# Differential attention's v projection moved into the stretch where GQA attention is woven with MLA, and new costs in the scheduler that orders the program

## The chip, the cores and the metric

One NeuronCore of a Trainium2 chip runs the whole kernel. It has a matrix engine (TensorE, "PE" in the rows), a vector engine (VectorE, DVE), a scalar engine (ScalarE, ACT), GpSimd (POOL), and SyncE (SP), which here issues the DMA transfers. Each engine works through its own instructions in the order in which the program has them, and waits for another through semaphores. The metric is the device time of one execution in microseconds. Less is better.

## The reference

Two requests of 512 and 256 tokens go through the same two-layer encoder trunk, of width 1024, in fp32. Cut to what matters:

```
def layer(x, c, l, p, pos, row, col):
    shift, scale, gate = split(silu(c) @ ada_w[l] + ada_b[l], 3)
    h = rms_norm(x, norm_g[l]) * (1 + scale) + shift
    qa, kva, kra, ga, qb, kb, vb, gb, xc, gc, qd, kd, vd, gd = split(h @ w_in[l])
    oa = mla_branch(qa, kva, kra, ...)   # latents normed, then up-projected to q, k, v; softmax attention
    ob = diff_branch(qb, kb, vb, ...)    # per head o1 - lam * o2, two softmax attentions with one v; rms_norm
    oc = rglru_branch(xc, ...)           # conv, two gates, linear recurrence in both directions
    od = gqa_branch(qd, kd, vd, ...)     # qk-norm, rotary, softmax attention, 4 q heads on 2 kv heads
    o = concat([oa*silu(ga), ob*silu(gb), oc*silu(gc), od*silu(gd)])
    return x + gate * (o @ w_out[l])

def trunk(x, c, p):            # once for the 512 tokens, once for the 256
    for l in range(2): x = layer(x, c, l, p, ...)
    return rms_norm(x, final_norm)
```

In the changed part `vb` is the 256 columns of `h @ w_in` that are differential attention's v.

## The kernel before

**Tiles.** The 768 tokens are six tiles of 128: group 0 has tiles 0 to 3 and group 1 has tiles 4 and 5. The normed input `h` stays in SBUF for a whole layer, with features on partitions, as eight chunks of 128 features. fp32 precision comes out of faster fp32r matmuls: each operand is split into a high part and a low rest, and `mm3` (its matmuls stand under L285) forms each product by three matmuls. A weight that arrives by DMA is split on chip: ACT copies the high part (`wh`) and DVE or POOL subtracts it to get the low part (`wl`, L211).

**Projections.** `token_chunk(ci)` projects one block of `w_in` to a token-major result, one token tile after the other, with 24 matmuls (8 chunks times 3) for each tile and one `yield` after it. Block 2 is differential attention's v (256 columns), 3 its q, 4 its k, and 5 MLA's latents (320 columns). `feat_tile` does the same for feature-major results: the RG-LRU input and the gates. `v_evac` brings a finished v tile from PSUM to SBUF, by two high copies on ACT and two subtractions on DVE (L460) for each tile.

**The program of a layer.** Work is written as generators, and `take` and `weave` interleave them. `weave(jobs, fill, per, ...)` writes an attention's jobs (scores, softmax, transposed probabilities, product with v) and, between them, steps of the generator `fill`. A fixed number, `F_D` for the first weave with one value for each layer, says how many steps come per job. The order of a layer is:

1. GQA's projections, whole;
2. GQA attention, filled with `mla()`: six tiles of latents, then up-projections;
3. MLA attention, filled with gate projections and the adaptive-norm weights;
4. RG-LRU and differential attention's projections by turns: `take(lru, 2)`, `take(df, 6)` (v), `take(lru, 2)`, `take(df, 6)` (q), `take(lru)`, `take(df)` (k). RG-LRU works in two halves of 128 channels, `ct` 0 and 1;
5. differential attention, filled with gates and weights; then the output projection.

**The order that runs.** The written order is only the input of `arrange`, a list scheduler that runs when the program is built. It takes, over all engines, the ready instruction that can start first by its own clock (between equals, the one written first), with `_cost` for the durations and `REACH` for the latency between engines. An instruction that opens a tile must find a free buffer of its pool (`acc` 2, `s` 2, `tr` 3 and `pv` 1 in PSUM; `ws` 4, `wh` 6 and `wl` 6 for weights), and a pool hands its buffers out in written order. The result fixes every engine's order, so a wrong cost shows as an engine that waits in order for something that comes late.

**Where things stand.** L520 is the softmax's row maximum on DVE, L764 differential attention's score matmuls, L622 the transposes of its rotated q and k, L460 and L463 (DVE) the low parts of what is brought out of PSUM. `stacks` then sends those to their places by small DMAs (L750, L752). The RG-LRU's sums are L993 to L1009 (DVE).

Of the kernel before, what the change touches and what calls it, by code (L numbers as in the profile page):

```python
# [10 lines left out]
F32 = mybir.dt.float32  # L11
# [3 lines left out]
AF = mybir.ActivationFunctionType  # L15
# [58 lines left out]
def body(ctx, tc, I, O, dbg=None):  # L74
# [312 lines left out]
    for l in range(DEPTH):  # L387
# [330 lines left out]

        def diff():
            both, Vs = v_tiles(4)  # L720

            def evac_v(tt, acc):
                v_evac(both, tt, acc)
            yield from token_chunk(2, evac_v)
            qr = sb([P, NT, 256], tag="rot")
            kr = sb([P, NT, 256], tag="rot")
# [28 lines left out]
            def job(g, cp, half, j, o, dens, after):  # L755
                n = GRP[g][1]
                st = {}

                def soft():
                    st["P"] = []  # L760
                    for h2 in range(n // 256):

                        (p1, d1), (p2, d2) = [softmax(
                            lambda out, qt: nc.tensor.matmul(out, q[:96, qt * P:(qt + 1) * P], k[:96], start=True,  # L764
                                                             stop=True), g, h2, d) for (q, k), d in
                            zip(st["qk"], (dens[:, 2 * h2:2 * h2 + 2, 2 * half + j], None))]
                        V.reciprocal(d2, d2)
                        V.scalar_tensor_tensor(d2, d2, nlam, d1, op0=ALU.mult, op1=ALU.mult)
                        for i in range(2):
                            V.scalar_tensor_tensor(p1[:, i], p2[:, i], d2[:, i:i + 1], p1[:, i],  # L770
                                                   op0=ALU.mult, op1=ALU.add)
                        st["P"].append(p1)
                        yield

                def pv():
                    yield from transpose_pv(st["P"], g, Vs[2 * half + j], lambda pv: o_evac(o, j, pv, n))
# [59 lines left out]

        def mla(ahead):
            lat = [pair(g) + pair(g) + pair(g) for g in range(2)]
# [30 lines left out]
            for tt, _ in enumerate(token_chunk(5, evac, ahead)):  # L869
# [193 lines left out]

        lru, gq = rglru(), gqa()
# [154 lines left out]
def _cost(i):  # L1219
# [6 lines left out]
    if kind == "InstMatmult":  # L1226
        n, cols, f32 = size(i.ins[0]), size(i.ins[1]), i.ins[0].dtype == F32
        if not f32:
            return max(n * 0.45 + 4, 118), n / 2.4 + 172
        if cols <= 64 and n > 128:  # L1230
            return n / 1.2 + 30, n / 0.6 + 160
        if n == 128:
            return 110, 273
        return (215, 362) if n < 128 else (n / 0.6 + 8, n / 0.6 + 170)
# [3 lines left out]
    if eng == mybir.EngineType.Activation:  # L1238
        s = 0.84 * n + (50 if psum else 92)
        if i.func not in (AF.Copy, AF.Square):  # L1240
            s += 110
        if len(outs) > 1:
            s += 90
        return s, s + 100
    if eng == mybir.EngineType.Pool:
        return 2.3 * n + 90, 2.3 * n + 135
    if kind in ("InstTensorScalarPtr", "InstTensorCopy") and not psum and len([a for a in ins if size(a) == n]) == 1:
        s = 0.66 * n + 70
    else:
        s = 1.04 * n + 65  # L1250
    return s, s + 80


REACH = {"PE": 54.0, "Activation": 35.0, "DVE": 33.0, "Pool": 78.0, "SP": 27.0}


def arrange(tc):
# [4 lines left out]
    for k, i in enumerate(prog):  # L1262
# [12 lines left out]
        for name, acc in touched.items():  # L1275
# [5 lines left out]
            users.setdefault(name, []).append(k)  # L1281
        deps.append(d - {k})
    users = {t: u for t, u in users.items() if tiles[t]._space != bass.MemoryType.DRAM}
    free, queue, opens, left = {}, {}, {}, {}
# [7 lines left out]
    for t, u in users.items():  # L1292
        for k in u:
            closes.setdefault(k, []).append(t)
    cost = [_cost(i) for i in prog]
    n = len(prog)
    after = [[] for _ in range(n)]
# [8 lines left out]
    at, came, end, freed = dict.fromkeys(REACH, 0.0), [0.0] * n, [0.0] * n, {}  # L1306
    dma, column, order = 0.0, None, []

    def buffers(k):
# [9 lines left out]
    while len(order) < n:  # L1319
        best = None  # L1320
        for e, ks in ready.items():
            for k in ks:
# [15 lines left out]
        if e == "PE":  # L1338
# [144 lines left out]
```

## Time and profile before

| | |
|---|---|
| runs of the kernel before | 964.23 us median of 3 (960.71 to 964.87) |
| profiled execution | 965.95 us, span 964.1 us |
| mean granted TensorE clock | 0.974 |
| PE busy | 889.8 us, 92% of the span |
| DVE busy | 730.8 us, 76% |
| ACT busy | 560.5 us, 58% |
| POOL busy | 153.7 us, 16% |

The span runs from the first to the last instruction of the profiled execution. "Busy" is the sum over an engine's instructions without overlaps. A matmul's end is modelled, so a row's duration is longer than the distance to the next matmul where they follow closely: the starts tell more than the durations.

### The profile page before, as it was taken

What the parts mean: (1) busy time and instruction counts of PE and PEld (TensorE: products, weight loads), DVE (VectorE), ACT (ScalarE), POOL (GpSimd) and SP (SyncE); (2) the same over time, 40 slices, a digit from 0 to 9 for tenths busy, and PEclk for the clock granted to TensorE, in tenths of its full rate; (3) what the DMA queues carried; (4) which work ended last, traced back from release to release, by engine and by line L of the source; (5) the groups of instructions that cost most, each with busy time, mean ns of one, the idle gap of its engine ahead of it and who ended that gap; (6) DMA issues with size and microseconds to landing.
All of it is one profiled execution on the core that took longest, in us unless ns stands there. A gap on an engine that the chain in (4) does not pass through costs nothing.

```text
span 964.1 us, 15513 instructions
## 1 busy us (share of the span) xinstructions
PE 889.8 (92%) x5248; PEld 726.4 (75%) x5248; DVE 730.8 (76%) x1894; ACT 560.5 (58%) x1355; POOL 153.7 (16%) x168
## 2 busy tenths in 40 slices
PE   4799989999999898998999999999999999998996
PEld 1598767686899566776888977777688887786785
DVE  5688988766498476879557899998556876998746
ACT  5544888766446354657336368988437535687412
POOL 0221011003121010113201111000032212010610
PEclk9899999999999798999999999999999999998999
DMA  9721012222202654236610112020331214323502
GB/s 347 264 72 55 1 66 66 65 61 84 66 23 80 178 161 161 68 88 240 222 56 34 45 55 66 2 66 18 106 108 45 66 59 123 94 59 129 175 23 109
DMA packets 54351, 91.72 MB, mean 95 GB/s; under 512 B 9072, under 2 KB 13936, under 8 KB 54272
## 3 DMA queue, kind: packets, MB, share of 16 engines
q1 hardware_dynamic: 54272, 90.73, 30.0%
q8 instruction: 42, 0.69, 0.3%
q14 instruction: 37, 0.30, 0.1%
HBM read 73.38 MB, written 6.31 MB: 83 GB/s over the span
## 4 chain that ended last, share of the span: by engine, by line
PE 49%; DVE 25%; ACT 11%; DMA 7%; issue 6%; SPq 1%; POOL 1%; DVEq 0%; ACTq 0%; POOLq 0%
PE acc L285 22%; PE tr L285 9%; PE s L285 7%; ACT p L114 4%; DVE mx L520 3%; PE pv L539 3%; DVE pt L460 2%; DMA b<-ada 2%; ACT b L114 2%; PE tr L535 2%; DVE p L770 2%; DVE b L460 2%; PE s L764 1%; DMA p<-x 1%; ACT tmp L114 1%
## 5 line engine op out<-in xcount | busy, mean ns | idle before, releaser
L285 PE MATMUL acc<-b,wh 128*128 128x512 f32 (+1 forms) x576 | 159.5, 358 | 0.0
L285 PE MATMUL acc<-wh,b 128*128 128x256 f32 (+4 forms) x720 | 158.0, 308 | 0.2 <-DVE b L1020 0.2
L211 POOL TENSOR_TENSOR wl<-ws,wh 128x512 fp32r<-128x512 f32 (+3 forms) x56 | 78.7, 1408 | 416.6 <-ACT wh L114 372.3
L114 ACT ACTIVATE p<-s,mx 128x512 f32<-128x512 f32 (+1 forms) x192 | 117.9, 616 | 46.0 <-DVE mx L520 37.1
L285 PEld LDWEIGHTS acc<-wh,b 128*128 128x128 f32 (+1 forms) x720 | 118.3, 190 | 3.8 <-DVE b L1020 1.2
L285 PE MATMUL acc<-wl,b 128*128 128x256 f32 (+4 forms) x360 | 112.7, 315 | 4.6 <-DVE rs_y L164 1.7
L285 PEld LDWEIGHTS acc<-b,wh 128*128 128x128 f32 x576 | 102.8, 195 | 13.5
L285 PE MATMUL acc<-b,wl 128*128 128x512 f32 (+1 forms) x288 | 104.3, 362 | 0.0
L520 DVE TENSOR_REDUCE mx<-s 128x1 f32<-128x512 f32 x128 | 86.4, 682 | 21.1 <-PE s L764 19.8
L539 PE MATMUL pv<-pt,b 128*128 128x512 f32 (+1 forms) x288 | 88.2, 393 | 8.8 <-DVE pt L460 7.5
L460 DVE TENSOR_TENSOR pt<-tr,pt 128x512 fp32r<-128x512 f32 (+1 forms) x144 | 84.2, 593 | 9.2 <-ACT pt L114 8.6
L114 ACT ACTIVATE pt<-tr 128x512 fp32r<-128x512 f32 (+1 forms) x144 | 74.2, 524 | 21.9 <-PE tr L535 21.1
L535 PE MATMUL tr<-c,p 128*128 128x128 f32 x480 | 77.9, 281 | 5.3 <-DVE p L770 2.5
L114 ACT ACTIVATE wh<-ws 128x512 fp32r<-128x512 f32 (+3 forms) x100 | 62.9, 636 | 32.6 <-PE tr L285 15.9
L285 PE MATMUL tr<-wh,b 128*128 128x256 f32 (+2 forms) x432 | 81.3, 288 | 0.0
L535 PEld LDWEIGHTS tr<-c,p 128*128 128x128 f32 x480 | 58.5, 143 | 24.5 <-DVE p L770 4.7
L285 PEld LDWEIGHTS acc<-wl,b 128*128 128x128 f32 (+1 forms) x360 | 68.1, 190 | 8.5 <-ACT pt L114 3.0
L539 PEld LDWEIGHTS pv<-pt,b 128*128 128x128 f32 x288 | 47.0, 193 | 34.9 <-DVE pt L460 22.4
L285 PEld LDWEIGHTS tr<-wh,b 128*128 128x128 f32 x432 | 67.4, 189 | 0.7
L285 PEld LDWEIGHTS acc<-b,wl 128*128 128x128 f32 x288 | 56.2, 195 | 8.1 <-issue 1.7
L285 PE MATMUL tr<-wl,b 128*128 128x256 f32 (+2 forms) x216 | 62.3, 288 | 0.0
L114 ACT ACTIVATE b<-tr 128x128 fp32r<-128x128 f32 (+7 forms) x92 | 39.5, 447 | 34.6 <-PE tr L622 11.6
(254 smaller groups left out, 1879.9 us busy)
## 6 DMA issues: line engine op xcount, KB each, us to landing
ws<-wf SPq DMA_DIRECT2D x40, 256.0 KB, 3.0
b<-ada SPq DMA_DIRECT2D x32, 256.0 KB, 5.4
ws<-wt SPq DMA_DIRECT2D x32, 256.0 KB, 2.9
wh<-ada SPq DMA_DIRECT2D x32, 256.0 KB, 3.5
wl<-ada SPq DMA_DIRECT2D x32, 256.0 KB, 3.7
ws<-wo SPq DMA_DIRECT2D x32, 256.0 KB, 2.7
b<-b SPq DMA_DIRECT2D x112, 64.0 KB, 2.0
b<-b SPq DMA_DIRECT2D x112, 32.0 KB, 1.9
```

The lines of the kernel that those rows point to most:

```text
L114: return nc.scalar.activation(out, in_, f, **kw)
L211: engine(eng).tensor_tensor(lo, w, hi.bitcast(F32), op=ALU.subtract)
L285: nc.tensor.matmul(out, s, m, start=first and i == 0, stop=last and i == 2)
L460: V.tensor_tensor(lo, src, hi.bitcast(F32), op=ALU.subtract)
L520: V.tensor_reduce(mx[:, i:i + 1], views[i], axis=AX.X, op=ALU.min)
L535: nc.tensor.transpose(tr[:, qt * P:(qt + 1) * P], Ps[qt // 2][:, qt % 2, kt * P:(kt + 1) * P], ident)
L539: nc.tensor.matmul(pv[:, :n], vt(g, kt), p[:, :n], start=(kt == 0 and i == 0), stop=(kt == nk - 1 and i == 1))
L764: lambda out, qt: nc.tensor.matmul(out, q[:96, qt * P:(qt + 1) * P], k[:96], start=True, stop=True), g, h2, d) for (q, k), d in
L770: V.scalar_tensor_tensor(p1[:, i], p2[:, i], d2[:, i:i + 1], p1[:, i], op0=ALU.mult, op1=ALU.add)
```

## The change

**The move.** v's projection becomes a generator of its own, `diff_v`. `mla` gets it as `between` and runs it after the latents of all six tiles and before the up-projections, so that it is written into GQA attention. `F_D` rises, since the fill has six steps more. In stage 4 the turns are now lru 2, q, lru 2, k, lru's rest: k's projection is written ahead of RG-LRU's last part.

**The scheduler's costs.** Several durations are refitted. A PE instruction whose operand comes late gets a penalty (`LOAD`, by its form), a transpose that another form follows gets 82 ns back, matmuls take longer while the scheduler believes the clock to be halved, and two instructions of DVE and POOL that touch only SBUF block each other (`shared`, `port`). The lines of the clock's model are left out below.

No instruction is added or removed: both programs have 5086 instructions on PE, 1896 on DVE, 1104 on ACT, 173 on POOL and 536 on SP.

```diff
-F_D, F_A, F_B, F_C = ((0.897, 1.178), (0.494, 0.213), (1.2, 1.393), (1.833, 0.976))
+F_D, F_A, F_B, F_C = ((1.4, 1.6), (0.494, 0.213), (1.2, 1.393), (1.833, 0.976))
...
-        def diff():
-            both, Vs = v_tiles(4)
+        def diff_v():
+            both, dv["Vs"] = v_tiles(4)
 
             def evac_v(tt, acc):
                 v_evac(both, tt, acc)
             yield from token_chunk(2, evac_v)
+
+        def diff():
             qr = sb([P, NT, 256], tag="rot")
...
-        def mla(ahead):
+        def mla(ahead, between):
...
+            yield from between
             qr = [sb([P, NT, 192], tag="rot") for _ in range(2)]
...
-        fill = mla(token_load(5) if PRE_D[l] else None)
+        fill = mla(token_load(5) if PRE_D[l] else None, vg)
...
         take(lru, 2)
         take(df, 6)
         take(lru, 2)
-        take(df, 6)
+        take(df)
         take(lru)
-        take(df)
...
+LOAD = {"r": 100.0, "t": 55.0, "n": 30.0, "c": 0.0}
...
-                key = (max(at[e], s + REACH[e] if s else 0.0), k)
+                r = s + REACH[e] if s else 0.0
+                if e == "PE":
+                    a = at[e] - (82 if pform == "t" != form[k][0] else 0)
+                    key = (max(a, r + LOAD[form[k][0]] if r > pst + 30 else 0.0), k)
+                else:
+                    key = (max(at[e], r), k)
...
+        elif shared[k]:
+            other = port["Pool" if e == "DVE" else "DVE"]
+            for a, b in other[-6:]:
+                if a < s + 60 < b:
+                    slot, took = max(slot, b - 140 + slot - s), max(took, b - 140 + took - s)
+            port[e].append((s, s + took))
```

**What moves: PE, layer 0, from MLA's latents to its first up-projection.** In the rows of an order a tile's name has its number; `acc_1770` is the last tile of latents, `kvl` and `kvh` are up-projection weights, and L704/L705 are GQA's scores. Before, the up-projection (`acc_1894`) follows the latents at once:

```order
L285 MATMUL acc_1770<-wl_1237,b_535 128x320
L285 MATMUL acc_1770<-wh_1235,b_535 128x320 x2
L285 MATMUL acc_1770<-wl_1237,b_543 128x320
L285 MATMUL acc_1770<-wh_1235,b_543 128x320 x2
...
L704 MATMUL s_1875<-b_1164,b_1170 128x256
L705 MATMUL s_1875<-b_1164,b_1170 128x256
L285 MATMUL acc_1894<-kvl_1846,b_1210 128x256
L285 MATMUL acc_1894<-kvh_1844,b_1211 128x256
L285 MATMUL acc_1894<-kvh_1844,b_1210 128x256
```

In the changed kernel v's matmuls (`acc_2106`, weights of 256 columns) stand in between, one by one between GQA attention's transposes (L535) and its scores, and the first up-projection (`acc_2178`) comes among the last of them:

```order
L285 MATMUL acc_2106<-wl_1784,b_503 128x256
L535 MATMUL tr_2152<-c_83,p_2018 128x128
L285 MATMUL acc_2106<-wh_1782,b_503 128x256
L535 MATMUL tr_2152<-c_83,p_2018 128x128
L285 MATMUL acc_2106<-wh_1782,b_503 128x256
...
L704 MATMUL s_2210<-b_1178,b_1184 128x256
L285 MATMUL acc_2106<-wl_1790,b_519 128x256
L285 MATMUL acc_2178<-kvl_1727,b_1194 128x256
L285 MATMUL acc_2106<-wh_1788,b_519 128x256
L285 MATMUL acc_2178<-kvh_1725,b_1195 128x256
```

All of v's 144 matmuls of a layer (6 tiles of 24) have left the stretch after MLA attention. Over the whole program, 570 of 780 transposes were followed by another transpose; now 83 are.

**DVE, layer 0, where differential attention begins.** L460 and L463 split the first transposed q and k, which `stacks` sends on by DMA; L1006 to L1009 (L1009 to L1012 in the changed kernel's numbering) are the end of RG-LRU's second half, with the sums in `b_3796` and `b_4006`; L735 to L740 rotate k. Before, the splits came after k's rotations, and RG-LRU had been done long before:

```order
L1008 SCALAR_TENSOR_TENSOR p_3730<-p_3731,p_3730 128x512
L1008 SCALAR_TENSOR_TENSOR p_3764<-p_3765,p_3764 128x256
L1009 TENSOR_TENSOR b_3796<-b_3796,p_3730 128x512
L1009 TENSOR_TENSOR b_3428<-b_3428,p_3764 128x256
...
L737 TENSOR_TENSOR t_947_4012<-rot_3514,c_85 128x64
L740 TENSOR_TENSOR rot_3514<-t_946_4010,t_947_4012 128x8x8
L460 TENSOR_TENSOR b_4026<-tr_4020,b_4025 128x512
L463 SCALAR_TENSOR_TENSOR b_4035<-tr_4029,b_4034 128x512
...
L520 TENSOR_REDUCE mx_4141<-s_4142 128x1
```

In the changed kernel they stand behind the last sums of RG-LRU, and L463 behind the very last:

```order
L1009 TENSOR_TENSOR p_3974<-p_3974,p_3973 128x512
L1011 SCALAR_TENSOR_TENSOR p_3940<-p_3941,p_3940 128x512
L1010 SCALAR_TENSOR_TENSOR b_3640<-p_3975,p_3974 128x256
L1012 TENSOR_TENSOR b_4006<-b_4006,p_3940 128x512
L1011 SCALAR_TENSOR_TENSOR p_3974<-p_3975,p_3974 128x256
L460 TENSOR_TENSOR b_4026<-tr_4020,b_4025 128x512
L1012 TENSOR_TENSOR b_3640<-b_3640,p_3974 128x256
L463 SCALAR_TENSOR_TENSOR b_4035<-tr_4029,b_4034 128x512
...
L520 TENSOR_REDUCE mx_4141<-s_4142 128x1
```

On PE, the transposes for these splits follow the last matmul of RG-LRU's second half at once. From that matmul to the first scores stand, in layer 0, 14 matmuls of 512 columns, 24 of 256, 8 transposes, and 8 matmuls of the adaptive norm (L226); in layer 1, 35 of 512, 26 of 256 and 16 transposes. Before, the transposes came right behind the last matmul of k, and RG-LRU's last matmul stood among k's first tiles.

**DVE, at the start.** L319 and L320 make the normed input's high and low parts, L233 to L247 compute the adaptive norm's scale and shift, L406 to L419 prepare small tables of layer 0, and L211 are low parts of weights. Before:

```order
L320 TENSOR_TENSOR b_377<-tmp_374,b_376 128x512
...
L233 COPY tmp_411<-acc_402 128x512
L241 TENSOR_TENSOR adaB_93<-tr_413,c_81 128x8
L406 TENSOR_TENSOR lp_559<-pt_549 128x64
...
L419 TENSOR_SCALAR subS_567<-subS_567 128x256
L233 COPY tmp_428<-acc_419 128x512
...
L211 TENSOR_TENSOR wl_595<-ws_591,wh_593 128x512
L245 TENSOR_TENSOR adaA_92<-tr_430,c_81 128x8
L246 TENSOR_SCALAR adaA_92<-adaA_92 128x8
```

In the changed kernel the tables stand ahead of L233, and two more weight splits (`wl_827`, `wl_833`) ahead of the last scale (L245):

```order
L406 TENSOR_TENSOR lp_559<-pt_549 128x64
L408 TENSOR_REDUCE ls_561<-lp_559 128x2
L400 TENSOR_TENSOR pt_554<-rot_551,pt_549 128x4x64
...
L419 TENSOR_SCALAR subS_567<-subS_567 128x256
L211 TENSOR_TENSOR wl_589<-ws_585,wh_587 128x512
...
L233 COPY tmp_411<-acc_402 128x512
L241 TENSOR_TENSOR adaB_93<-tr_413,c_81 128x8
L233 COPY tmp_428<-acc_419 128x512
L211 TENSOR_TENSOR wl_827<-ws_823,wh_825 128x576
L211 TENSOR_TENSOR wl_833<-ws_829,wh_831 128x576
L245 TENSOR_TENSOR adaA_92<-tr_430,c_81 128x8
L246 TENSOR_SCALAR adaA_92<-adaA_92 128x8
```

## Rows read from the trace of the kernel before

**Rows 1.** The page's busy times: engine, us (share of the span), number of instructions.

```profile
PE 889.8 (92%) x5248; PEld 726.4 (75%) x5248; DVE 730.8 (76%) x1894; ACT 560.5 (58%) x1355; POOL 153.7 (16%) x168
```

**Rows 2.** Busy times by stretch: us; PE, PEld, DVE, ACT, POOL; PEclk, DMA, GB/s.

```profile
83.00:152.00 69.00, 62.34 (x371) 50.88 (x369) 63.91 (x222) 55.07 (x159) 8.54 (x15) 1.00 0.14 43
152.00:228.80 76.80, 74.31 (x422) 55.11 (x423) 58.61 (x135) 54.60 (x136) 8.08 (x17) 1.00 0.25 73
228.80:311.30 82.50, 79.44 (x591) 74.34 (x590) 61.22 (x119) 42.87 (x85) 18.08 (x16) 1.00 0.18 55
556.00:632.00 76.00, 69.71 (x412) 58.17 (x411) 70.49 (x249) 60.25 (x178) 10.42 (x22) 0.98 0.14 44
632.00:702.50 70.50, 68.13 (x381) 49.15 (x379) 53.01 (x111) 49.91 (x123) 6.26 (x11) 1.00 0.22 67
702.50:783.00 80.50, 78.28 (x583) 73.39 (x581) 60.27 (x110) 43.51 (x82) 19.23 (x17) 1.00 0.20 60
```

**Rows 3.** The chain that ended last, 236 to 260 us: start, us, what.

```profile
240.21 2.84 PE acc L285 x24
...
254.75 0.30 DVE b L460
```

**Rows 4.** PE's timeline, the last matmuls of RG-LRU's second half, layer 0.

```profile
295.78 0.62 PE L285 MATMUL tr<-b,pt 128*128 128x256 f32 x3
```

**Rows 5.** DVE's timeline, layer 0: RG-LRU's last sums, and the second split.

```profile
307.24 1.00 DVE L1009 TENSOR_TENSOR b<-b,p 128x512 f32<-128x512 f32 x2
...
313.46 0.68 DVE L463 SCALAR_TENSOR_TENSOR b<-tr,b 128x512 fp32r<-128x512 f32 x1
```

**Rows 6.** The page's DMA issues: count, KB each, us to landing.

```profile
b<-b SPq DMA_DIRECT2D x112, 64.0 KB, 2.0
```

**Rows 7.** PE's timeline, start of differential attention, layer 0: start, us, line, tiles, shapes.

```profile
311.39 1.04 PE L622 MATMUL tr<-c,rot 128*128 128x128 f32 x8
312.18 0.47 PE L285 MATMUL acc<-b,wl 128*128 128x512 f32 x1
312.49 0.62 PE L285 MATMUL acc<-b,wh 128*128 128x512 f32 x2
312.95 0.40 PE L285 MATMUL acc<-b,wl 128*128 128x512 f32 x1
...
324.41 1.19 PE L764 MATMUL s<-b,b 96*128 96x512 f32 x2 [3.60 <-DMA b<-b]
```

**Rows 8.** PE's timeline at the start: the adaptive norm's matmuls (L226) and last row sums.

```profile
29.53 2.26 PE L226 MATMUL acc<-b,c 128*32 128x512 f32 x16
...
39.49 1.57 PE L236 MATMUL tr<-c,tmp 128*128 128x2 f32 x8 [4.28 <-DVE tmp L233]
```

**Rows 9.** PE's timeline, start of differential attention, layer 1; in brackets idle time and releaser.

```profile
786.19 0.33 PE L622 MATMUL tr<-c,rot 128*128 128x128 f32 x1 [2.16 <-DVE rot L740]
```

**Rows 10.** Busy times by stretch, two stretches at half clock; columns as in rows 2.

```profile
323.10:340.10 17.00, 15.34 (x46) 9.08 (x47) 8.57 (x17) 5.34 (x14) 0.00 (x0) 0.50 0.62 191
...
787.00:791.00 4.00, 4.00 (x12) 3.10 (x12) 2.51 (x7) 1.44 (x2) 0.00 (x0) 0.57 0.48 161
```

**Rows 11.** PE's timeline, 47 us on: transposes (L312) between matmuls.

```profile
47.14 0.28 PE L285 MATMUL s<-wh,b 128*128 128x256 f32 x1
47.26 0.38 PE L312 MATMUL tr<-c,p 128*128 128x128 f32 x2
47.39 0.36 PE L285 MATMUL s<-wh,b 128*128 128x256 f32 x1
47.59 0.28 PE L285 MATMUL s<-wl,b 128*128 128x256 f32 x1
```

**Rows 12.** DVE's timeline, same start in layer 1: rotations during POOL's splits, and after.

```profile
784.58 1.30 DVE L737 TENSOR_TENSOR t<-rot,c 128x64 f32<-128x64 f32 x1
...
786.31 0.22 DVE L737 TENSOR_TENSOR t<-rot,c 128x64 f32<-128x64 f32 x1
```

**Rows 13.** POOL's timeline, same start in layer 1.

```profile
781.88 3.92 POOL L211 TENSOR_TENSOR wl<-ws,wh 128x512 fp32r<-128x512 f32 x3 [18.14 <-ACT wh L114]
```

More of the change, by code (lines that the diff above doesn't have):

```diff
@@ L775, in pv @@
                 def pv():
-                    yield from transpose_pv(st["P"], g, Vs[2 * half + j], lambda pv: o_evac(o, j, pv, n))
+                    yield from transpose_pv(st["P"], g, dv["Vs"][2 * half + j], lambda pv: o_evac(o, j, pv, n))
                     after()
@@ L1062, in weave @@
                     next(fill, None)
-        lru, gq = rglru(), gqa()
+        dv = {}
+        lru, gq, vg = rglru(), gqa(), diff_v()
         rot_acc[:] = ROT_A
@@ L1228, in _cost @@
         if not f32:
[L1229 removed]
+            return max(n * 0.443 + 4, 117), n / 2.4 + 172
         if cols <= 64 and n > 128:
[L1231 removed]
+            return n / 1.2 + (55 if cols == 64 else 8), n / 0.6 + 160
         if n == 128:
[L1233 removed]
+            return 109, 273
         return (215, 362) if n < 128 else (n / 0.6 + 8, n / 0.6 + 170)
@@ L1238, in _cost @@
     if eng == mybir.EngineType.Activation:
-        s = 0.84 * n + (50 if psum else 92)
-        if i.func not in (AF.Copy, AF.Square):
-            s += 110
+        s = 0.845 * n + (64 if psum else 98)
+        if i.func == AF.Identity or i.func in (AF.Exp, AF.Tanh) and not psum:
+            s += 185
+        elif i.func in (AF.Exp, AF.Tanh):
+            s += 89 if i.func == AF.Exp else 44
         if len(outs) > 1:
-            s += 90
+            s += 92
         return s, s + 100
     if eng == mybir.EngineType.Pool:
-        return 2.3 * n + 90, 2.3 * n + 135
-    if kind in ("InstTensorScalarPtr", "InstTensorCopy") and not psum and len([a for a in ins if size(a) == n]) == 1:
-        s = 0.66 * n + 70
+        return 2.38 * n + 80, 2.38 * n + 125
+    single = len([a for a in ins if size(a) == n]) == 1 and not psum
+    if kind == "InstTensorCopy" and single:
+        s = 0.545 * n + 68
+    elif kind == "InstTensorScalarPtr" and single:
+        s = 0.62 * n + 78
     else:
-        s = 1.04 * n + 65
+        s = 1.03 * n + 78
     return s, s + 80
 REACH = {"PE": 54.0, "Activation": 35.0, "DVE": 33.0, "Pool": 78.0, "SP": 27.0}
+LOAD = {"r": 100.0, "t": 55.0, "n": 30.0, "c": 0.0}
+WINDOW = 3413.0
 def arrange(tc):
@@ L1295, in arrange @@
     cost = [_cost(i) for i in prog]
+    form, shared = [None] * n_prog, [False] * n_prog
+    for k, i in enumerate(prog):
+        if eng[k] == "PE":
+            w, f32 = int(np.prod([c for _, c in i.ins[0].ap[1:]])), i.ins[0].dtype == F32
+            form[k] = "r" if not f32 else "t" if w == P else "n" if w < 32 else "c", w * (2 if f32 else 1) / 2.4
+        elif eng[k] in ("DVE", "Pool"):
+            shared[k] = not any(hasattr(a, "ap") and a.bass_ap.tensor._space == bass.MemoryType.PSUM
+                                for a in list(i.ins) + list(i.outs))
     n = len(prog)
@@ L1307, in arrange @@
     dma, column, order = 0.0, None, []
+    port = {"DVE": [], "Pool": []}
+    pst, pform, slow, busy, wend = -1e9, None, 2.0, 0.0, WINDOW
     def buffers(k):
@@ L1343, in arrange @@
                 s += 92
-            column = (pos, s + took - 10) if pos else None
+            fm, beats = form[k]
+            while s >= wend:
+                slow = (1.0 if busy >= 0.46 * WINDOW else 2.0) if slow == 1 else (1.0 if busy >= 0.81 * WINDOW else 2.0)
+                busy, wend = 0.0, wend + WINDOW
+            slot, took = slot + (slow - 1) * beats, took + (slow - 1) * beats
+            column = (pos, s + took - 10) if pos else None
+            pst, pform = s, fm
+            x = s
+            while s + slot > wend:
+                busy += wend - x
+                slow = (1.0 if busy >= 0.46 * WINDOW else 2.0) if slow == 1 else (1.0 if busy >= 0.81 * WINDOW else 2.0)
+                x, busy, wend = wend, 0.0, wend + WINDOW
+            busy += s + slot - x
+        elif shared[k]:
[4 more added lines that the diff above has]
+            port[e].append((s, s + took))
         if e == "SP":
```

1 line of the change is left out of this document (added).

## The prediction

> **What bounds the kernel now.** I read the page's busy times first, then busy times by stretch, then the chain that ended last, then PE's and DVE's timelines where a stretch begins. The page shows PE busy for 889.8 us [rows 1]; the profiled execution took 965.95 us. No other engine is near that, so PE's stream of matmuls and the places where it waits make the time. The stretches say where it waits [rows 2]. In layer 0, the one with GQA attention and MLA (83 to 228.8 us) leaves PE idle for 6.66 + 2.49 = 9.15 us; the one with RG-LRU's and differential attention's projections (228.8 to 311.3) for 3.06 us. In layer 1 the same stretches show 6.29 + 2.37 = 8.66 us and 2.22 us. The early part of the attention stretch, where the latents and up-projections hang on each other, is also DVE's fullest: 63.91 of 69 us, and 70.49 of 76 in layer 1. So the change takes work out of a nearly dense stretch and puts it into one with gaps. What it is worth depends on how much of it falls into these gaps, and on what the dense stretch was hiding.
>
> **v's matmuls leave the projections.** The chain passes through v's tiles whole, at 2.84 us for each 24 matmuls [rows 3]. Six tiles are 17.0 us in each layer, all on the path that sets the end: -34.0 us.
>
> **They arrive in GQA attention.** They need only `h` and weights, so they can stand in any gap where PE would wait for a softmax or a latent, and they put 144 matmuls between latents and up-projections, which wait for each other today. Their evacuation is 12 subtractions on DVE of 0.30 us [rows 3], 3.6 us beside 126 of it in 155 us, and is hidden. Two bounds. If every idle microsecond is filled, the stretch grows by 17.0 - 9.15 = 7.85 us in layer 0 and 8.34 in layer 1. If it only gets as dense as the projections are now, 79.44 of 82.5, or 96.3%, its 136.65 + 17 us of PE's work take 159.6 us, which is 13.8 more than now; in layer 1 (137.84 + 17 at 78.28 of 80.5, 97.2%) 12.7 more. PE's busy time counts modelled ends, so the second bound is too dark. I take 9.5 us each, nearer to the first, because the new matmuls depend on nothing that is late: +19.0, between 16.2 and 26.5. The move's net is -15.0, between -17.8 and -7.5.
>
> **The start of differential attention.** This is what the dense stretch was hiding. Before, RG-LRU's second half ended under k's projection: its last matmuls ended at 296.40 [rows 4], its last sums at 308.24 [rows 5], 11.8 us later, with PE busy throughout. Now k is projected first. The orders show the transposes of q and k right behind RG-LRU's last matmul, and on DVE both low-part splits behind its last sums. So the splits end 11.8 + 0.68 + 0.68 = 13.2 us after that matmul. The transfers that bring the split parts to their places follow. One takes 2.0 us from issue to landing [rows 6]; the order has two more at SP behind it before the scores' tiles are whole, and I add half as much again for these: 3.0 us, an estimate. The first scores can start 16.2 us after RG-LRU's last matmul. PE has this much to do until then: in layer 0, 14 x 0.23 + 24 x 0.118 + 8 x 0.10 us [rows 3, 7] is 6.9, and 8 matmuls of the adaptive norm cost between 0.14 (16 of them in 2.26 us, four at a time [rows 8]) and, alone among others, perhaps 0.5 each. That makes 8.0 to 10.9, and I take 9.5. PE waits 6.7 us, where it waited 3.60 [rows 7]: +3.1. In layer 1, 35 x 0.23 + 26 x 0.118 + 16 x 0.10 is 12.7 us, so it waits 3.5, where it waited 2.16 [rows 9]: +1.3. The half clock that follows such a wait is there already, 17.0 us at 0.50 in layer 0 and about 3.4 us at half in layer 1 [rows 10]; I add nothing for it. Below, the bound is no extra wait (0); above, the transfers take what they took in layer 0 before, from the second split's end at 314.14 [rows 5] to 324.41 [rows 7], 10.3 us. Sum: +4.4, between 0 and +19.0.
>
> **RG-LRU's sums.** In the projections DVE keeps 61.22 us [rows 2], less the 3.6 of v, in 17 us less: 57.6 of 65.5, 88%. That is less full than the early attention stretch (93%), where PE still ran at 90%, and part of the sums moves behind the stretch. I take +0.5 each: +1.0, between 0 and +4.
>
> **The costs: transposes.** Of 780 transposes 570 were followed by another, now 83. The scheduler spreads them because it gives 82 ns back when another form follows. The trace shows both halves of this. After eight transposes the next matmul starts early: 0.79 us after the first one, so some 28 ns after the last. But the matmul after that comes 0.31 us later, where 0.23 is plain [rows 7]: what was won is paid at once. Between matmuls of 256 columns, two matmuls and two transposes take 0.45 us, from 47.14 to 47.59 [rows 11]; with 0.118 for a matmul that leaves 0.107 for a transpose, about as much as in a dense row of them. So spreading 487 transposes gains nothing, and what two decimals leave open, 5 ns each, is 2.4 us either way. I take +1.2, because a spread order splits chains that ran dense, between -2.4 and +4. The Trainium skill (TensorE: Matmul & The Clock Gate, Step-by-step: what each phase is for) says the same against this cost: in a stream a matmul takes as long as its moving columns need, whatever stands next. By it the term is 0; by the constant in the code it would be -39.9.
>
> **The costs: POOL and DVE.** In layer 1 the last rotation of k before differential attention took 1.30 us, where the same operation takes 0.22 a moment later [rows 12]; three splits of weights ran on POOL then, 1.31 us each [rows 13]. The 2.16 us wait of PE [rows 9] comes from it. A scheduler that knows this can put other work there; the gain is inside the +1.3 above. The Trainium skill (SBUF — State Buffer, Who interferes with whom) has such a rule: a DVE instruction with two SBUF inputs contends with one of GpSimd that reads SBUF. The trace agrees (1.30 against 0.22). v's weights bring two POOL splits per layer into the stretch where DVE is fullest; the fourth rival prices them.
>
> **The start-up.** The order puts the small tables ahead of the adaptive norm's copies on DVE and two more weight splits ahead of its last scale. PE already waited 4.28 us for the last of those copies [rows 8]. It comes later now; against it three tiles of the first projections can start on the half that is ready. I take +1.0, between -1 and +4.
>
> **The sum.** -15.0 + 4.4 + 1.0 + 1.2 + 1.0 = -7.4, from 965.95 to 958.55. The profiled execution stands 1.7 us above the median of the runs, so I forecast 956.8. That the new costs shuffle every other stretch too (nearly every row of DVE's order stands elsewhere) has no price in any row; it widens the range by some 2 us on both sides.
>
> **Rivals.**
> 1. *The gain stays in the attention stretch.* It gets only as dense as the projections: -7.5 instead of -15.0, sum +0.1, 964.3 us. For it: the dark bound is what a tuned stretch reaches here. Against it: those stretches wait inside chains, where v has none.
> 2. *Slower by the first softmax.* The transfers need 10.3 us, because weight loads are in the queues ahead of them as they were in layer 0. PE waits 14.0 us in layer 0 (+10.4) and 10.8 in layer 1 (+8.6), and layer 1 gets a half clock as long as layer 0's, 17.0 instead of 3.4 us, +6.8. That is +25.8 in place of 4.4: +14.0, and 978.2 us. It decides when the two starts cost over 16.6 us together, since the sum is then over +4.8.
> 3. *Spread transposes are really cheaper*, 487 x 0.082 = -39.9 instead of +1.2: 915.7 us. The starts [rows 7, 11] speak against it.
> 4. *POOL blocks DVE in the fullest stretch.* Four splits of 1.31 us hold up DVE by about 1.1 each, all of it on the path: +4.4, which gives 961.2 us. For it: DVE is at 93%. Against it: v's subtractions read PSUM, and the softmax's long operations do so too.
>
> **How the numbers follow.** The time can be told from no change only beyond 0.5%, below 959.4 or above 969.1. Forecast 0.49, rival 1 0.16, rival 2 0.14, rival 3 0.03, rival 4 0.10; 0.08 for start-up and shuffled stretches that cost over 10 us together, at some 972. The forecast's own range, 945 to 962, has its lower end at -17.8 for the move, 0 for the starts, -1 for the start-up and 2 us of shuffle (945.6) and its upper end where the starts cost half their bound; about a fifteenth of it lies over 959.4 and counts as no change, as does rival 4. Faster 0.49 - 0.02 + 0.03 = 0.50 and same 0.16 + 0.10 + 0.02 = 0.28 leave slower 0.22. The range for 8 in 10 leaves out rival 3, most of rival 2, and goes from 943 to 973, with the shuffle's 2 us below and the smaller mishaps above.
>
> **What would show it.** In the changed kernel's trace: v's matmuls (256 columns, `wt` weights) before the first up-projection in each layer; the GQA and MLA stretch longer by 8 to 14 us, the projections shorter by 16 to 17; PE's waits before the first scores of differential attention near 6.7 and 3.5 us, with DMA or DVE named; transposes and matmuls that alternate at 0.107 and 0.118 us. I am wrong if the attention stretch grows by the full 17 us, if the first scores wait over 10 us, or if the starts of alternating transposes are 30 ns apart without the next matmul paying for it.

## The result: slower by 2.9%, and where the time went

The changed kernel takes 991.22 us (median of 4 runs, 990.84 to 992.25), the kernel before 964.55 us beside it. The ratio is 1.0287, with a 95% interval of 1.0259 to 1.0315. The prediction was 956.8, with a range of 943 to 973.

The page of the changed kernel hardly says why. PE is busy for 28.5 us more than in [rows 1], and its share of the span hardly changes (93% against 92%):

```profile
PE 918.3 (93%) x5248; PEld 734.5 (74%) x5248; DVE 727.6 (73%) x1894; ACT 565.1 (57%) x1355; POOL 150.5 (15%) x168
```

PE has the same 5248 matmuls and needs longer for them. The busy times by stretch (columns as in [rows 2]) show where. They are GQA and MLA attention (from the first latent), the projections (to k's last matmul) and differential attention of layer 0, then the same of layer 1.

```profile
84.10:251.50 167.40, 159.46 (x940) 125.92 (x939) 130.26 (x377) 118.55 (x312) 19.53 (x34) 1.00 0.19 58
251.50:314.60 63.10, 59.82 (x429) 56.39 (x428) 43.24 (x93) 24.67 (x49) 13.22 (x14) 0.97 0.22 67
314.60:444.40 129.80, 123.06 (x578) 81.42 (x578) 95.71 (x186) 75.42 (x174) 13.67 (x10) 0.95 0.41 120
564.20:735.80 171.60, 159.75 (x932) 128.26 (x930) 133.40 (x384) 119.33 (x319) 17.55 (x31) 0.95 0.18 55
735.80:797.00 61.20, 57.92 (x423) 54.61 (x423) 42.81 (x84) 24.55 (x45) 17.49 (x19) 1.00 0.21 62
797.00:900.50 103.50, 93.14 (x505) 76.10 (x503) 87.46 (x173) 71.80 (x169) 11.34 (x9) 0.94 0.29 78
```

The projections shrink by 19.4 and 19.3 us: v's 144 matmuls are gone, and in each layer 20 of RG-LRU's last ones now stand behind k's. The attention stretches took 145.5 and 146.3 us before; they grow by 21.9 and 25.3 us, both more than the 17.0 us that came in. The first suspect is one line, L226, the adaptive norm's matmuls. These are its busy times alone (PE's, then PEld's), in the same three stretches, first of the kernel before, then of the changed one:

```profile
83.30:228.80 145.50, 7.38 (x32) 1.02 (x32) 1.00 0.19 59
311.60:434.00 122.40, 14.00 (x64) 2.03 (x64) 0.89 0.45 133
556.20:702.50 146.30, 7.17 (x32) 1.12 (x32) 0.99 0.18 55
```

```profile
84.10:251.50 167.40, 16.73 (x32) 2.20 (x32) 1.00 0.19 58
314.60:444.40 129.80, 26.18 (x64) 3.48 (x64) 0.95 0.41 120
564.20:735.80 171.60, 13.61 (x32) 1.81 (x32) 0.95 0.18 55
```

The same 128 matmuls (64 instructions of two passes each) cost 9.35 + 12.18 + 6.44 = 28.0 us more. The timeline of PE in the changed kernel shows how:

```profile
203.21 0.27 PE L535 MATMUL tr<-c,p 128*128 128x128 f32 x1
203.41 1.04 PE L226 MATMUL acc<-wh,c 128*32 128x512 f32 x2
204.39 0.33 PE L535 MATMUL tr<-c,p 128*128 128x128 f32 x1
...
205.46 1.04 PE L226 MATMUL acc<-wl,c 128*32 128x512 f32 x2
206.43 0.96 PE L285 MATMUL s<-b,b 96*128 96x512 f32 x3
```

Each of these instructions uses 32 of the array's 128 columns (128*32). Alone among others, its two passes hold PE for 0.98 us, from 203.41 to 204.39. In the kernel before most of them stand together. Over the whole program, with 32 more of these instructions at the start, the kernel before has 28 groups, 9 of them a single instruction; the changed kernel has 69 groups, 62 of them single. Behind the start 49 of the 64 stand alone, where 8 did.

At the start the scattering costs next to nothing: L226 holds PE there for 26.17 us instead of 17.11, and the first latent comes 0.8 us later. That suggests that its price depends on whether PE would have waited otherwise.

### The profile page after: what moved, and what is told of

The parts are those of the page before. It is cut to its first block, busy times and chain, and to the rows that moved or that the text cites. A ratio compares the mean times of both kernels' runs of the same rounds, so it can differ in the third digit from the quotient of the medians.

```text
span 990.4 us, 15585 instructions
## 1 busy us (share of the span) xinstructions
PE 918.3 (93%) x5248; PEld 734.5 (74%) x5248; DVE 727.6 (73%) x1894; ACT 565.1 (57%) x1355; POOL 150.5 (15%) x168
## 3 DMA queue, kind: packets, MB, share of 16 engines
q1 hardware_dynamic: 54272, 90.73, 29.5%
## 5 line engine op out<-in xcount | busy, mean ns | idle before, releaser
L285 PE MATMUL acc<-wh,b 128*128 128x256 f32 (+4 forms) x816 | 211.3, 318 | 0.0
L285 PE MATMUL acc<-b,wh 128*128 128x512 f32 (+1 forms) x576 | 180.6, 379 | 0.0
L285 PEld LDWEIGHTS acc<-wh,b 128*128 128x128 f32 (+1 forms) x816 | 147.7, 191 | 4.8 <-issue 0.6
L211 POOL TENSOR_TENSOR wl<-ws,wh 128x512 fp32r<-128x512 f32 (+3 forms) x56 | 77.3, 1382 | 461.3 <-ACT wh L114 258.4
L285 PE MATMUL acc<-wl,b 128*128 128x256 f32 (+4 forms) x408 | 127.9, 322 | 12.0 <-DVE wl L211 6.6
L535 PE MATMUL tr<-c,p 128*128 128x128 f32 x480 | 118.6, 281 | 5.2 <-DVE rs_t L162 1.5
L460 DVE TENSOR_TENSOR pt<-tr,pt 128x512 fp32r<-128x512 f32 (+1 forms) x144 | 85.2, 596 | 25.6 <-ACT pt L114 24.1
L285 PEld LDWEIGHTS acc<-wl,b 128*128 128x128 f32 (+1 forms) x408 | 76.7, 191 | 18.6 <-DVE wl L211 7.4
L535 PEld LDWEIGHTS tr<-c,p 128*128 128x128 f32 x480 | 66.9, 143 | 24.6 <-issue 10.2
L114 ACT ACTIVATE wh<-ws 128x512 fp32r<-128x512 f32 (+3 forms) x100 | 62.7, 636 | 37.1 <-PE tr L285 11.7
L539 PEld LDWEIGHTS pv<-pt,b 128*128 128x128 f32 x288 | 52.4, 201 | 15.8 <-DVE pt L460 4.1
L285 PE MATMUL s<-b,b 96*128 96x512 f32 (+2 forms) x192 | 58.9, 405 | 0.6 <-DMA b<-b 0.6
L211 DVE TENSOR_TENSOR wl<-ws,wh 128x512 fp32r<-128x512 f32 (+2 forms) x44 | 35.8, 816 | 22.1 <-ACT wh L114 22.1
```

Of the source, the lines that this page charges most:

```text
L114: return nc.scalar.activation(out, in_, f, **kw)
L211: engine(eng).tensor_tensor(lo, w, hi.bitcast(F32), op=ALU.subtract)
L285: nc.tensor.matmul(out, s, m, start=first and i == 0, stop=last and i == 2)
L460: V.tensor_tensor(lo, src, hi.bitcast(F32), op=ALU.subtract)
L535: nc.tensor.transpose(tr[:, qt * P:(qt + 1) * P], Ps[qt // 2][:, qt % 2, kt * P:(kt + 1) * P], ident)
L539: nc.tensor.matmul(pv[:, :n], vt(g, kt), p[:, :n], start=(kt == 0 and i == 0), stop=(kt == nk - 1 and i == 1))
```

## The experiments

All were compared with the kernel before on the same chip, where that took 961 to 963 us. "Groups" are those of L226.

| run | program | costs | us | ratio to before (95%) |
|---|---|---|---|---|
| e1 | moved | old | 967.24 | 1.0059 (1.0035 to 1.0083) |
| e2 | old | new | 993.21 | 1.0323 (1.0279 to 1.0368) |
| e3 | moved | new, small ones together | 970.63 | 1.0078 (1.0051 to 1.0105) |
| e4 | moved | new, no chain term | 978.74 | 1.0169 (1.0118 to 1.0219) |
| e5 | moved, old turns | old | 973.84 | 1.0116 (1.0088 to 1.0144) |
| e6 | moved, v among up-projections | old | 977.27 | 1.0155 (1.0129 to 1.0181) |
| e7 | old | old, small ones together | 965.38 | 1.0016 (0.9993 to 1.0038) |
| e8 | old | new, small ones together | 962.03 | 1.0002 (0.9976 to 1.0027) |
| e9 | old, short v | old | 959.77 | 0.9965 (0.9936 to 0.9994) |
| e10 | moved, short v | old | 955.35 | 0.9925 (0.9895 to 0.9954) |
| e11 | moved | new, without two terms | 959.24 | 0.9967 (0.9938 to 0.9995) |
| e12 | old | new, together after the start | 964.09 | 1.0023 (0.9997 to 1.0049) |
| e13 | moved, faster fill | old | 966.69 | 1.0056 (1.0036 to 1.0076) |
| e14 | old | new, without two terms | 949.63 | 0.9879 (0.9846 to 0.9911) |

**e1 and e2: which half of the change costs it.** e1 is the changed program with `_cost` and `arrange` of before; e2 is the program of before with `_cost` and `arrange` of the changed kernel.

> The moved program with the scheduler's costs of before. Its order keeps the adaptive norm's small matmuls (L226, 32 columns of the array) in 27 groups, as before (28), where the changed kernel has 69. Theory A (the new costs scatter these matmuls, each group takes about 0.98 us whether it holds one or four, 41 more groups cost some 26 us; the move itself is worth little): 955 to 968 us. Rival B (the move costs it: v does not fit into GQA attention, and differential attention starts late): 980 to 990 us.

> The program of before, without the move, with the new costs of the scheduler. Its order has 69 groups of the adaptive norm's matmuls, 63 of them single. Theory A: 985 to 993 us. Rival B (the move costs it): 960 to 968 us.

e1 took 967.24 us and e2 993.21. The slowdown is in the costs: without the move they cost 3.2%. The move costs 0.6% by itself, and should have gained 15 us.

**e3 and e4: how the costs do it.** e3 adds to the changed kernel only this:

```diff
-                    a = at[e] - (82 if pform == "t" != form[k][0] else 0)
+                    a = at[e] - (82 if pform == "t" != form[k][0] else 0) + (900 if pform == "c" != form[k][0] else 0)
```

> The changed kernel, with one more term in the scheduler: another form after one of the adaptive norm's matmuls is put 900 ns later. Its order has 10 groups of them instead of 69, all else of the new costs is kept. Theory A: the 26 us come back, 962 to 969 us. Rival B: 983 to 991 us.

e4 keeps the other new terms and takes the penalty out of accumulations (`fed` is false where a matmul waited last for its own predecessor on PE; the lines that set it are left out):

```diff
-                    key = (max(a, r + LOAD[form[k][0]] if r > pst + 30 else 0.0), k)
+                    late = r + LOAD[form[k][0]] if fed[k] else s
+                    key = (max(a, late if late > pst + 30 else 0.0), k)
```

> The changed kernel, where the penalty for late operands no longer counts for the next matmul of the same accumulation, so that such chains are not split for it; 50 groups of the adaptive norm's matmuls, 41 of them single. Theory A: with 19 of the 41 extra groups gone, 976 to 984 us. Rival C (what costs time is that two accumulations alternate matmul by matmul): 960 to 968 us.

e3 took 970.63, 21 us less than the changed kernel; e4 978.74, 12 us less. Both are in theory A's range or 2 us beside it, and rival C's range is missed. In e3's timeline on PE the eight instructions of a chunk stand together; four passes on the four quarters of the array start 10 ns apart, and all sixteen take 1.85 us, from 195.66 to 197.51, where eight instructions alone take 8 x 0.98 = 7.84:

```profile
195.37 0.36 PE L285 MATMUL acc<-b,wh 128*128 128x256 f32 x1
195.66 0.62 PE L226 MATMUL acc<-wh,c 128*32 128x512 f32 x1
195.67 0.62 PE L226 MATMUL acc<-wl,c 128*32 128x512 f32 x1
...
196.11 0.59 PE L226 MATMUL acc<-wh,c 128*32 128x512 f32 x1
...
197.51 0.39 PE L539 MATMUL pv<-pt,b 128*128 128x256 f32 x1
```

The Trainium skill (TensorEngine Tiling (Array Packing), Key Properties) says that tiles of the array work independently, and that a change of the tiling mode drains TensorE. The trace agrees: the first starts 0.29 us after a matmul of 256 columns, where 0.12 is plain, and four run at once.

**e11 and e14: the two terms out.** e11 is e4 without the 82 ns as well; e14 puts these costs on the program of before.

```diff
-                    a = at[e] - (82 if pform == "t" != form[k][0] else 0)
+                    a = at[e]
```

> The changed kernel without both terms that put another form after a matmul: no penalty inside an accumulation (as e4) and no 82 ns back after a transpose. Its order has 32 groups of the small matmuls. Theory G (these two terms scatter them, and nothing else in the new costs matters much): 960 to 970 us. Rival (the refitted durations or the other terms cost too): 975 us or more.

> The program of before with the costs of e11 (new, without the two terms). Against e11 it is the move alone under these costs. Theory (the move costs about what e1 showed, 5 us): 952 to 957 us. Rival (under these costs the move gains or is worth nothing): 958 to 964 us.

e11 took 959.24 us with 32 groups, 0.8 us under theory G's range: the two terms together scatter the small matmuls. A matmul of 256 columns holds PE for 118 ns, but its successor in the same accumulation is ready only after 154 ns by the scheduler's clock, so anything else goes first; so it is behind a transpose, by the 82 ns. e14 took 949.63 us, 2 us under its range. It is the fastest version here: the refitted durations and the other terms are worth 1.2%, and the move takes 959.24 - 949.63 = 9.6 us of it away.

These two runs also give the move at equal costs, from one trace of each (us, layers 0 and 1; the last column has what the prediction's terms for that stretch add up to over both layers):

| stretch | e14, old place | e11, moved | difference | forecast |
|---|---|---|---|---|
| first latent to the projections | 145.0, 145.6 | 157.3, 157.7 | +24.4 | +19.0 |
| projections, to the last matmul of k or of RG-LRU | 82.4, 83.4 | 66.2, 70.1 | -29.5 | -33.0 |
| from there to the first scores | 13.0, 17.7 | 20.0, 23.0 | +12.3 | +4.4 |

But scattering isn't all that the two terms cost. e3 keeps both terms and the small matmuls together. Behind the start these hold PE for 16.43 us in e3 and for 34.43 in e11, and yet e3 takes 970.63 us, 11.4 more than e11. In the old place it is the same: e12 (15.39 us of L226, see below) takes 964.09 and e8 (17.15) 962.03, where e14 (33.75) takes 949.63. So from the kernel before to the changed one the runs lead by -11.6 (e14), +9.6 (the move, e11), +11.4 (the two terms without the scattering, e3) and +20.6 us (the scattering). Some of the 11.4 is lost at the start: the first latent comes at 86.7 us in e3, at 84.1 in the changed kernel and at 81.8 in e11. What makes the rest was not tried; the median granted clock of the runs is 0.961 in e3 and 0.970 in e11, 0.970 in e12 and 0.983 in e14.

**e7, e8 and e12: fewer groups than before.** e7 and e8 have e3's term in the kernel before and in e2; e12 has it after the first four chunks only. In e7 it reads (`thin` holds L226's instructions, `small` is true behind one of them; the lines that set them are left out):

```diff
-                key = (max(at[e], s + REACH[e] if s else 0.0), k)
+                key = (max(at[e] + (900 if e == "PE" and small and k not in thin else 0), s + REACH[e] if s else 0.0), k)
```

> The kernel before, with nothing but the term that keeps the adaptive norm's small matmuls together: 9 groups instead of 28. Theory A: groups behind the start fall from 30.6 us to about 20, so 952 to 957 us. Rival (before, they stood in waits of PE and cost nothing): 960 to 965 us.

> The program of before with the new costs, and the small matmuls kept together (9 groups instead of e2's 69). Theory A: 993.2 of e2 less 27 to 35, 958 to 966 us. Rival (other new costs, such as two accumulations in turn, cost as much): 973 us or more.

> As e8, but the small matmuls are kept together only after those of the start, where e8 lost 6 us before the latents of layer 0. Theory: those 6 us come back, 954 to 959 us, under the kernel before. Rival (the half clock or the shuffle eats them): 960 to 965 us.

e8 got back all that e2 had lost, 31 us. But e7 gained nothing over before, though L226's busy time behind the start fell from 28.55 to 17.10 us:

```profile
100.00:980.00 880.00, 17.10 (x128) 3.51 (x128) 0.97 0.27 84
```

So theory A falls, and the rival's number came (0.4 us over its range), but its reason isn't shown. In e7's trace 4.3 us were lost ahead of the latents of layer 0 (87.6 instead of 83.3), from there to layer 1's first scores 7.8 us were gained, and behind these, where no L226 stands, 3.6 us were lost. e12 took 964.09, so its theory falls as well: the first latent is back at 84.3 us, from 89.5 in e8, but the time is not.

**e5: the turns.** RG-LRU's rest stands ahead of k again (its second pair of steps, ahead of q before, now stands behind q with it):

```diff
-        take(lru, 2)
-        take(df)
         take(lru)
+        take(df)
```

> The move with the old costs, and with the old turns: RG-LRU's rest is written before k again. Theory D (RG-LRU's second half behind k makes differential attention start late in layer 1, where the time of e1 that PE's matmuls do not explain grew from 20.0 to 28.0 us): 8 us below e1, 957 to 962 us. Rival (the loss there is the half clock's chance and not the turns): 964 to 970 us.

It took 973.84 us, more than e1: theory D falls as a remedy, and the rival's range is missed too. The wait only changed its place. In e1, where k comes first, PE waits at the start of differential attention (first of layer 0, then of layer 1):

```profile
329.52 1.06 PE L226 MATMUL acc<-wh,c 128*32 128x512 f32 x1 [10.07 <-DVE tmp L483]
...
798.57 1.11 PE L622 MATMUL tr<-c,rot 128*128 128x128 f32 x4 [8.20 <-DVE b L460]
```

In e5 it waits inside the projections, in k's tiles:

```profile
297.59 0.58 PE L285 MATMUL acc<-wl,b 128*128 128x256 f32 x1 [7.30 <-DVE rot L193]
```

```profile
763.69 0.58 PE L285 MATMUL acc<-wl,b 128*128 128x256 f32 x1 [7.24 <-DVE rot L193]
```

DVE works in order, and e1's DVE shows what stands ahead: RG-LRU's last scans and sums (L1011, L1012), then the splits, and only then the evacuation (L483) that frees PE's next buffer.

```profile
324.98 1.77 DVE L1011 TENSOR_TENSOR_SCAN p<-p,p 128x512 f32<-128x512 f32 x2
326.68 1.00 DVE L1012 TENSOR_TENSOR b<-b,p 128x512 f32<-128x512 f32 x2
327.59 0.68 DVE L460 TENSOR_TENSOR b<-tr,b 128x512 fp32r<-128x512 f32 x1
328.19 0.68 DVE L463 SCALAR_TENSOR_TENSOR b<-tr,b 128x512 fp32r<-128x512 f32 x1
328.79 1.00 DVE L483 SCALAR_TENSOR_TENSOR tmp<-tmp,acc 128x512 f32<-128x512 f32 x2
```

**e9 and e10: what v's matmuls cost in either place.** `token_chunk` sums one chunk of features for block 2:

```diff
-                for k in range(KC):
+                ks = range(1 if ci == 2 else KC)
+                for k in ks:
...
```

> The kernel before, where v's projection sums one of eight feature chunks only: 126 of v's 144 matmuls of each layer are left out, 29.7 us of PE's work, so v is not the reference's. In the dense projections v should cost its whole length: 930 to 936 us.

> The move with the old costs, with the same 126 matmuls of v left out in each layer (v is not the reference's). Theory F (v costs its full length in GQA attention too, the gaps there are not filled by it): 29.7 us under e1, 934 to 941 us. Rival (half of v falls into gaps, as the prediction had it, and e1 loses elsewhere): some 13 to 15 us under e1, 951 to 955 us.

Taking 29.7 us of matmuls out of the dense projections saves 961.23 - 959.77 = 1.5 us by the medians, 3.4 us by the ratio (0.35%, interval 0.06 to 0.64). In e9's two projection stretches PE's idle time is 11.1 and 10.8 us, where it was 3.06 and 2.22 [rows 2], and the granted clock is 0.91:

```profile
229.60:309.90 80.30, 69.17 (x466) 62.85 (x465) 59.48 (x122) 42.09 (x85) 16.04 (x16) 0.91 0.19 58
696.10:774.90 78.80, 68.04 (x459) 62.01 (x457) 58.45 (x113) 42.87 (x82) 16.38 (x17) 0.91 0.20 61
```

These are its waits of PE in layer 0 over 1 us (L461 is what was L460, as one line was added), and an instruction of DVE that the first one waits behind:

```profile
245.60 0.55 PE L285 MATMUL acc<-wl,b 128*128 128x256 f32 x1 [2.81 <-DVE b L461]
248.31 0.76 PE L285 MATMUL acc<-b,wl 128*128 128x512 f32 x1 [1.74 <-DVE b L461]
...
287.44 3.57 PE L285 MATMUL tr<-b,pt 128*128 128x512 f32 x9 [5.07 <-DVE rot L193]
```

```profile
243.99 0.28 DVE L461 TENSOR_TENSOR b<-acc,b 128x128 fp32r<-128x128 f32 x1
```

The first two are made by the test itself. A v tile takes three matmuls there, but still its two subtractions on DVE, and for these PE waits: 4.5 us in layer 0 and 5.4 in layer 1. The third, 5.1 us in each layer, is for DVE's copies of q's tiles (L193), behind the rotations of q and splits of weights. And the matmuls that are left get longer: the nine at 287.44 take 3.57 us, 0.40 each where 0.23 is plain, at a granted clock of 0.50, the lower of the two levels (1.2 of 2.4 GHz). PE's busy time falls by 10.3 and 10.2 us in the two stretches, though 14.85 us of matmuls left each. So e9 doesn't say what v as a whole, with its evacuation, cost in its old place; the table above, where all of it leaves, says more.

In the new place the same omission saves 967.24 - 955.35 = 11.9 us of 29.7, near the rival's 13 to 15: theory F falls. How much of the rest v fills in gaps isn't shown, since v's evacuation stays here too and PE's busy time falls by 19.5 us only (862.3 instead of 881.8).

**e6 and e13: could the attention stretch take v better?** In e1 these are the latents, v, and the up-projections in GQA and MLA attention of layer 0:

```profile
82.80:124.00 41.20, 39.29 (x233) 33.88 (x232) 36.89 (x134) 29.00 (x84) 5.76 (x9) 0.96 0.11 33
124.00:158.00 34.00, 32.84 (x237) 29.69 (x237) 25.78 (x78) 24.63 (x63) 4.25 (x5) 1.00 0.14 43
158.00:178.00 20.00, 17.02 (x104) 14.01 (x102) 15.95 (x60) 16.08 (x54) 3.16 (x11) 1.00 0.27 85
```

v's part is dense (32.84 of 34.0), the up-projections behind it leave 3 us. e6 puts three tiles of v among the up-projections:

```diff
-            yield from between
+            for _ in range(3):
+                next(between)
+                yield
...
+                    if tt % 2 == 0:
+                        next(between)
+                        yield
+            take(between)
```

> The move with the old costs, but only three tiles of v stand before MLA's up-projections, the other three among them. Theory E (v did not fill PE's waits, it took the up-projections' place as cover, and these now wait at the start of MLA attention): the two stretches of GQA and MLA attention get 3 to 5 us shorter each than in e1, 957 to 963 us. Rival (DVE and ACT bound these stretches, whatever stands where on PE): 965 to 970 us.

e13 only raises the pace, for each layer:

```diff
-F_D, F_A, F_B, F_C = ((1.4, 1.6), (0.494, 0.213), (1.2, 1.393), (1.833, 0.976))
+F_D, F_A, F_B, F_C = ((2.0, 2.3), (0.494, 0.213), (1.2, 1.393), (1.833, 0.976))
```

> The move with the old costs, with F_D at 2.0 and 2.3 instead of 1.4 and 1.6, so that the fill (latents, v, up-projections) is written earlier into GQA attention. Theory H (v pushed the up-projections out of GQA attention, and its tail no longer covers them): the stretches of GQA and MLA attention get 3 to 6 us shorter each than in e1, 956 to 962 us. Rival (DVE, at 92% there, sets the length whatever the pace): 965 to 972 us.

e6 took 977.27 us and e13 966.69: theories E and H fall, both rivals' numbers or worse came. In e10, where v's matmuls are nearly gone, the same stretch of GQA attention shows DVE at 24.88 of 27.0 us:

```profile
123.00:150.00 27.00, 20.59 (x109) 16.18 (x108) 24.88 (x76) 23.03 (x65) 4.15 (x5) 0.81 0.25 82
```

That fits the rival, DVE as the limit under v; it was not tried by taking work from DVE.

## Why the prediction was wrong

**The small matmuls: the term that was missing.** "That the new costs shuffle every other stretch too (nearly every row of DVE's order stands elsewhere) has no price in any row; it widens the range by some 2 us on both sides" is the sentence that failed. I counted what the order did to transposes and not what it did to L226. I even had the price nearly at hand: [rows 8] gave 0.14 us for a pass in a group, and I put a single one at "perhaps 0.5 each" in one place only, where I also took 8 instructions for 8 passes. Single, an instruction's two passes take 0.98 us, 0.49 each. If all 64 instructions behind the start cost that, it would be 62.7 us; 49 stand alone, and 56.5 were measured, where it was 28.55 before. e2 (+3.2%), e3 and e8 (21 and 31 us back) show it as the largest cause. The same sentence hid two more: what the two terms cost besides (11.4 us, its cause open) and what the refitted durations gave back (11.6 us).

**v's matmuls leave the projections: -34.0.** Nearly right for the stretch itself, which got 29.5 us shorter in e11 than in e14. What was wrong is "all on the path that sets the end": of that, the first scores, which now wait for RG-LRU's chain on DVE, took 12.3 us back.

**They arrive in GQA attention: +19.0.** Right in kind, but too small. In e11 against e14 (same costs, small matmuls in 32 and 33 groups) the stretch of layer 0 grew by 157.3 - 145.0 = 12.3 us, between the two bounds of 7.85 and 13.8, and that of layer 1 by 12.1:

```profile
82.30:227.30 145.00, 134.04 (x792) 107.14 (x791) 122.21 (x356) 110.02 (x293) 16.85 (x31) 0.99 0.19 59
```

```profile
81.70:239.00 157.30, 148.60 (x935) 123.40 (x935) 126.26 (x371) 115.78 (x310) 19.39 (x34) 1.00 0.20 61
```

The bound from how dense the projections are was not too dark but nearly right. With the old costs (e1) the stretches grew by 16.5 and 13.3 us, over the range's 26.5 together, and in the changed kernel by 21.9 and 25.3, of which the small matmuls are 9.35 and 6.44; without these, the full 17 us that I had named as a sign of being wrong came in layer 1 alone (18.9).

**The start of differential attention: +4.4.** The chain was right, but too short: at equal costs the start grew by 12.3 us. Another instruction waits than the one I named: mostly not the scores for a transfer, but a matmul or transpose for a buffer, whose evacuation stands behind RG-LRU's sums on DVE. DVE's splits end 14.2 to 16.8 us after RG-LRU's last matmul (changed kernel, e1 and e11), where I had 13.2, and the first scores start 17.0 to 24.2 us after it, where I had 16.2. These are the longest waits in layers 0 and 1 of the changed kernel, then of e11; forecast were 6.7 and 3.5 us:

```profile
339.56 0.77 PE L285 MATMUL acc<-b,wl 128*128 128x512 f32 x1 [3.88 <-DVE tmp L483]
...
821.48 0.38 PE L285 MATMUL acc<-b,wl 128*128 128x256 f32 x1 [3.81 <-DVE tmp L483]
```

```profile
321.44 1.06 PE L226 MATMUL acc<-wh,c 128*32 128x512 f32 x1 [9.09 <-DVE tmp L483]
...
785.46 1.12 PE L622 MATMUL tr<-c,rot 128*128 128x128 f32 x4 [5.96 <-DVE b L460]
```

That the changed kernel's wait in layer 0 is short is luck: the scores come 19.5 us after RG-LRU's last matmul, but the scattered small matmuls fill the time, and PE has 15.5 us to do there instead of 9.5. With the old costs the waits were 10.07 and 8.20 (e1), between the forecast and the second rival's 14.0 and 10.8; over the 3.60 and 2.16 of before that is 12.5 us, less than the 16.6 at which that rival was to decide.

**Transposes: +1.2.** Right. In the changed kernel a matmul starts 0.03 us after a transpose, and the next transpose 0.23 us after that matmul:

```profile
119.88 0.27 PE L535 MATMUL tr<-c,p 128*128 128x128 f32 x1
119.91 0.40 PE L285 MATMUL acc<-wh,b 128*128 128x320 f32 x1
120.14 0.27 PE L535 MATMUL tr<-c,p 128*128 128x128 f32 x1
```

A pair takes 0.26 us, which is what the plain distances (0.15 and 0.11) add up to. So the 82 ns are paid back, as [rows 7] and [rows 11] had it. The third rival is out. The fourth has no sign in the trace: in the two attention stretches the DVE instructions that run beside POOL's and last over 0.2 us longer than the median of their shape do so by 7.7 us in sum, 8.7 before.

**Start-up and RG-LRU's sums: +1.0 each.** The latents of layer 0 begin at 84.1 us instead of 83.3, as forecast to 0.2 us, though the small matmuls' 9.1 us more there weren't in the sum. RG-LRU's sums I had taken as hidden; they are what e1 and e5 wait for.

**What stays open.** In layer 1 of the changed kernel the attention stretch grew by 25.3 us, of which v's 17.0 and the small matmuls' 6.4 leave 1.9, so no gap was filled there on balance, and the granted clock there is 0.95 where it was 0.98 and 1.00 [rows 2]. Why it fell in that layer and not in layer 0 wasn't tried. Nor was the last step of why the move loses 5 to 10 us shown: that DVE's chains under PE bound the start of differential attention and GQA attention fits e5 and e10, but no run took work from DVE. And what the two scheduler terms cost beside the scattering is open.

## What to carry to other kernels

A dense engine on the chain is not yet worth its length: before a block is moved out, ask which wait becomes due behind it (here the projections got 29.5 us shorter and the start behind them 12.3 us longer). A test that shortens the block on one engine alone can make waits of its own, as e9 did: take out what the block costs the other engines too. When a scheduler's costs change, count in the new order every kind of instruction whose price depends on its neighbours, not only the kind that the change names; here 64 instructions on a quarter of the array, set apart, cost more than any other part of the diff. And try the halves of a change apart: one half here was a gain of 1.2% (e14), hidden under two of its own terms and the move.

## What the runs showed of the hardware

A matmul on 32 of 128 columns costs PE as much alone (0.98 us for its two passes, changed kernel at 203.41 us) as in a group of four on the four quarters (0.98 to 1.00 us for eight passes), and eight together take 1.85 us for sixteen (e3). In e3 the first of them starts 0.29 us after a matmul on the whole array, where 0.12 is plain. And less work on PE may come with a lower clock: in e9, with 29.7 us less to do and longer waits, the two projection stretches ran at a granted clock of 0.91 where it had been 1.00.
